# Seven-product groups and GpSimd lower parts in the down projection of a two-layer encoder trunk

## The chip, the cores and the metric

The kernel runs on one core of a Trainium2 chip. A core has a matrix engine (TensorE, PE in the profile; PEld is its weight load), a vector engine (VectorE, DVE), an activation engine (ScalarE, ACT), a general engine (GpSimd, POOL) and a queue engine that starts most transfers (SyncE, SP). Matmuls accumulate in PSUM, eight banks of 128 x 512 float32 values; everything else lies in SBUF. The metric is the time of one execution on the device in microseconds.

## The reference

The input is one sequence of 256 tokens with 2048 features. There are two layers. Layer 0 mixes tokens with a convolution module, layer 1 with latent attention. After each comes the same MLP:

```
def sq_relu_mlp(h, w1, w2):
    return jnp.square(jax.nn.relu(h @ w1)) @ w2

    for layer in range(DEPTH):
        h = rms_norm(x, norm_mixer_g[layer])
        x = x + (conv_module(h, ...) if layer % 2 == 0 else mla(h, ...))
        h = rms_norm(x, norm_mlp_g[layer])
        x = x + sq_relu_mlp(h, mlp_w1[layer], mlp_w2[layer])
    return rms_norm(x, final_norm_g)
```

All tensors are float32. `mlp_w1` is 2048 x 8192 and `mlp_w2`, the down projection, 8192 x 2048, for each layer.

## The kernel before

**Products in three terms.** TensorE multiplies in a reduced format (`F32R`). To keep float32's accuracy each operand is split into an upper part (`hi`, a rounding copy on ScalarE, L168 and L489) and a lower part (`lo = raw - hi`, a subtraction, L172 and L490). A product is then three matmuls, `hi*hi + lo*hi + hi*lo` (`mm3`, L201 to L203). Every weight that comes from memory therefore passes through ScalarE and one more engine before TensorE can use it. `load` fetches a block of weights of 512 KB or 1 MB into one of three `raw` buffers; `split` makes the two parts in two halves of 128 x 1024, in rings of six `hi` and six `lo` buffers (`WB`).

**The MLP** (`mlp`) handles the 8192 inner features in two halves. A half has an up stage and a down stage. The up stage makes eight groups of 512 inner features: matmuls at L615 and L616, then the squared ReLU on VectorE (L634 to L637) and its split into `gh`, `gl`. The down stage multiplies these with `mlp_w2`, for two blocks of 512 output columns at a time (`Sums`, here called a column pair), and adds the result to the residual `xs`. Each half has two column pairs, so the kernel has eight.

**Plain and mixed groups.** A plain pair of 128-row chunks of the inner dimension, against two row tiles of tokens and two column blocks, takes 8 products, 24 matmuls (`Sums.plain`). A mixed pair takes 7 products, 21 matmuls (`Sums.mixed`), after Strassen's scheme in Winograd's form. For that the weights are combined first (`mixed_weights`): VectorE makes one subtraction of 128 x 1024 (L497) and two of 128 x 512 (L498, L499) on the raw weights, and seven matrices have to be split instead of four: three lower parts of 1024 columns and one of 512, all on VectorE (L490). The activations are combined likewise in the up stage (`mixed_inputs`). `MIXED` names the mixed groups of each layer and half: 0, 2, 4 in three of them, 0 and 2 in layer 0's second half. They have buffers of a larger shape (`sh`, `sl`, `N_MIXED` of each).

**Order.** A column pair holds all eight PSUM banks: four shared sums `u` and four ends `e`. Mixed and plain pairs alternate while there are mixed ones; then come the rest of the plain ones. Ahead of the last plain pair stands `join`, which combines the `u` banks into the residual: one copy on ScalarE and eight additions on VectorE. The last column pair of a half is run differently (`product_A` with `beside=between`): there the plain groups come as blocks of four chunks by 512 columns, and in the very last stage the last block's last three groups are worked through once per row tile, so that the first tile's final norm can begin early (`finish`, `before`). `turns_on` takes a few small steps from a list (transposes of the residual on VectorE for the next layer's input) behind each pair. The engines work through their queues in order; the order of the MLP's instructions is made by a scheduler from the order of the program.

**Elsewhere.** In the convolution stage the lower parts of `conv_w_pw1` are made by GpSimd (L172), and so are some additions; VectorE sums filter taps there, with the running sum in PSUM (L848). In the attention GpSimd turns the rotary part of the queries (L1317 to L1322, L1530). `w_dw`, the table of filter taps, lies in the pool of constants; `gf`, the final gain, has a pool of its own that is open during the last MLP.

Of the kernel before, what the change touches and what calls it, by code (L numbers as in the profile page):

```python
# [10 lines left out]
F32 = mybir.dt.float32  # L11
# [4 lines left out]
ALU = mybir.AluOpType  # L16
AX = mybir.AxisListType

P = 128
D = 2048  # L20
# [13 lines left out]
KR = 512  # L34
CHUNK = 64
HALVES = 2
PAD_CONST = 24
PAD_SMALL = 48
PAD_RIGHT = 48
PAD_KV = 8  # L40
PAD_O = 56
WB = 6
LOOK = WB // 2 - 1
MIXED = {(0, 0): (0, 2, 4), (0, 1): (0, 2), (1, 0): (0, 2, 4), (1, 1): (0, 2, 4)}
N_MIXED = 3


SIDE = {KC - 3: 2, KC - 2: 4}
# [29 lines left out]
def trunk_kernel(  # L78
# [323 lines left out]

    def product_A(
        w, k_lo, nk, hi, lo, add, prepare, blocks=range(NNB), due=(), finish=None, before=None,
        groups=None, banks=None, begun=None, beside=None,
    ):

        due = list(due)
        groups = list(range(nk // 4)) if groups is None else groups
        begun = set() if begun is None else begun  # L410
        nu = len(groups)

        def first(ps):
            fresh = id(ps) not in begun
            begun.add(id(ps))
            return fresh

        for n in blocks:
            ps = [acc_tile() for _ in range(T)] if banks is None else banks[n]

            n_end = 3 if finish is not None and n == blocks[-1] else 0
            wjs = []

            def products(u, t, to_end=True):
                for j in range(4):
                    mm3(
                        ps[t], hi(4 * groups[u] + j, t), lo(4 * groups[u] + j, t), *wjs[u](j),
                        first(ps[t]), u == nu - 1 - (not to_end) and j == 3,
                    )

            for u, g in enumerate(groups):
                wjs.append(load_split([rows(w, k_lo + 4 * g, 4, n * NB, NB)], 4))
                if u < nu - n_end:
                    for j in range(4):
                        k = 4 * g + j
                        for t in range(T):
                            mm3(ps[t], hi(k, t), lo(k, t), *wjs[u](j), first(ps[t]), u == nu - 1 and j == 3)
                if banks is None:
                    while due:
                        prepare(due.pop(0))  # L440
                    step(-(-20 * 4 // nk) + 1 if nk > 4 * NNB else 6)
                else:
                    turns_on(due, prepare)
                if u == 0 and n_end:
                    before()
                if beside is not None:
                    beside(n, u, due)
            if n_end:
                for t in range(T):


                    halves = t == T - 1
                    for u in range(nu - n_end, nu - halves):
                        products(u, t, not halves)
                    add(n, ps, t)
                    if not halves:
                        prepare(n, t)
                    else:
                        h = NB // 2
                        for c in range(2):  # L460
                            o = acc_tile()[:, :h]
                            for j in range(4):
                                k = 4 * groups[-1] + j
                                wh, wl = (w[:, c * h : (c + 1) * h] for w in wjs[-1](j))
                                mm3(o, hi(k, t), lo(k, t), wh, wl, j == 0, j == 3)
                            add(n, {t: o}, t, c)
                            prepare(n, t, c)
                    finish(t)
            else:
                for t in range(T):  # L470
                    add(n, ps, t)
                due.append(n)
        while due:
            prepare(due.pop(0))

    def turns_on(due, prepare, n=4):

        if due and not steps:
            prepare(due.pop(0))
        step(n)  # L480
# [42 lines left out]
    class Sums:  # L523
# [25 lines left out]

        def plain(self, w, k, hi, lo, k0, end):  # L550

            at_j = split(load([rows(w, k, 2, self.n * NB, 2 * NB)], 2), nc.vector)
            order = [(j, c, t) for j in range(2) for c in range(2) for t in range(T)]
            if end:
                order.sort(key=lambda r: r[1:])
            for j, c, t in order:
                wh, wl = (a[:, c * NB : (c + 1) * NB] for a in at_j(j))
                ps = self.e[t][c]
                mm3(ps, hi(k0 + j, t), lo(k0 + j, t), wh, wl, self.first(ps), end and j == 1)

        def join(self, pool):

            u1, u6, u7, u5 = self.u
            x = lambda t, c: xs[:, t, (self.n + c) * NB : (self.n + c + 1) * NB]
            a, b = (pool.tile([P, 2, S], F32, tag="v", name=nm("v"), bufs=2).rearrange("p a n -> p (a n)") for _ in range(2))
            tt = nc.vector.tensor_tensor
            nc.scalar.activation(a, u1, AF.Copy)
            tt(x(0, 0), u1, x(0, 0), op=ALU.add)
            tt(a, u6, a, op=ALU.add)
            tt(b, u7, a, op=ALU.add)  # L570
            tt(a, u5, a, op=ALU.add)
            tt(x(1, 0), b, x(1, 0), op=ALU.add)
            tt(b, u5, b, op=ALU.add)
            tt(x(0, 1), a, x(0, 1), op=ALU.add)
            tt(x(1, 1), b, x(1, 1), op=ALU.add)

    def mlp(layer, ssq, next_gain, finish=None, before=None, beside=None):

        with ExitStack() as cx:
            mp = cx.enter_context(tc.tile_pool(name=f"mp{layer}", bufs=1, reuse_waits="tile"))  # L580
# [16 lines left out]
            for hf in range(HALVES):  # L597
# [4 lines left out]
                for g in range(ng):  # L602
# [17 lines left out]
                    if beside is not None and g == 2:  # L620
                        beside(mp)
                        beside = None
                    if g in mixed or len(mixed) < N_MIXED and g == plain[-1]:
                        shape = [P, 2, 7, P] if g in mixed else [P, 4, S]
                        gs[g] = [mp.tile(shape, F32R, tag=f"s{c}", name=nm(f"s{c}"), bufs=N_MIXED) for c in "hl"]
                    else:
                        gs[g] = [mp.tile([P, 4, S], F32R, tag=f"g{c}", name=nm(f"g{c}"), bufs=ng - N_MIXED) for c in "hl"]
# [29 lines left out]
                for n in range(0, NNB - 2 * last, 2):  # L657
                    sums = Sums(n)
                    ks = [4 * g + 2 * b for g in plain for b in range(2)]
                    for i, k in enumerate(ks):  # L660
                        if i < len(ms):
                            mixed_quad(sums, i)
                            turns_on(due, prepare)
                        if i == len(ks) - 2:
                            sums.join(mp)
                        sums.plain(w, k_lo + k, hi, lo, k, i == len(ks) - 1)
                        turns_on(due, prepare)
                    for c in range(2):
                        for t in range(T):
                            add(n + c, [sums.e[i][c] for i in range(T)], t)  # L670
                        if last:
                            due.append(n + c)
                if last:
# [2 lines left out]

                    def between(n, u, due):
                        if n == n2 and u < len(plain) - 1:
                            lo_i, hi_i = (len(ms) * i // (len(plain) - 1) for i in (u, u + 1))
                            for i in range(lo_i, hi_i):  # L680
                                mixed_quad(sums, i)
                                turns_on(due, prepare)
                        if n == n2 and u == len(plain) - 1:
                            sums.join(mp)

                    product_A(
                        w, k_lo, nkh, hi, lo, add, prepare, range(n2, NNB), due,
                        finish=(lambda t: finish(nssq, t)) if finish is not None else None,
                        before=lambda: before(nssq),
                        groups=plain, banks={n2 + c: [sums.e[t][c] for t in range(T)] for c in range(2)},  # L690
                        begun=sums.begun, beside=between,
                    )
            return nssq

# [1 line left out]
    with ExitStack() as cx:  # L696
# [1 line left out]
        cv2 = cx.enter_context(tc.tile_pool(name="cv2", bufs=2, reuse_waits="tile"))  # L698

        NW = W * KC // 4  # L700
        w_dw = const.tile([P, W * KC], F32, name="w_dw")

        X_PARTS = [(0, D // 2, 3 * D // 4, D), (0, D // 2, 7 * D // 8, D)]
        X_PARTS = [list(zip(c, c[1:])) for c in X_PARTS]
# [1055 lines left out]
        product_A(mla_w_o[0], 0, H, oh_kt, ol_kt, add, prepare, range(2, NNB), range(2))  # L1760


    with tc.tile_pool(name="fin", bufs=1, reuse_waits="tile") as fp:
        gf = fp.tile([P, D], F32, name="gf")
        nc.scalar.dma_start(gf, final_norm_g.rearrange("(a n) -> a n", a=1).partition_broadcast(P))

        def gained(t, n):
            sl = slice(n * NB, (n + 1) * NB)
            nc.vector.tensor_tensor(xs[:, t, sl], xs[:, t, sl], gf[:, sl], op=ALU.mult)

        def finish(ssq, t):

# [17 lines left out]
            for i, (c0, c1) in enumerate(zip(cuts, cuts[1:])):  # L1790
                ob = xs[:, t, c0:c1]
                if c1 == D:
                    nc.vector.scalar_tensor_tensor(
                        out=ob, in0=ob, scalar=y, in1=gf[:, c0:c1], op0=ALU.mult, op1=ALU.mult
                    )
                elif i in (1, 3):
                    nc.scalar.activation(ob, ob, AF.Copy, scale=y)
# [20 lines left out]
                for n in range(NNB - 1):  # L1818
                    gained(t, n)

        mlp(1, ssq, None, finish, before)


_INS = [
# [23 lines left out]
```

## Time and profile before

| what | us |
|---|---|
| median of 3 runs | 1955.66 (1955.34 to 1955.98) |
| profiled execution | 1955.42 |
| its span, from the first to the last instruction | 1953.6 |
| TensorE busy | 1932.2 |
| VectorE busy | 1547.1 |
| ScalarE busy | 1058.6 |
| GpSimd busy | 220.5 |

The granted TensorE clock was 0.998. A row of the groups names line, engine, operation, output and inputs, shape and count, then busy time, the mean of one in ns, and the idle time of the engine just before such instructions with what ended it. A row of the order of time has start and length in us, engine, line, operation, operands, count, and in brackets the idle time ahead of it. A matmul's own length is its latency; as they are pipelined, the distance from one to the next is shorter.

### The profile page before, as it was taken

The numbers are of one execution on the slowest core, as the hardware profiler recorded it, in microseconds if no ns is written. First come the engines' busy times: TensorE is split into PE (matmuls) and PEld (weight loads), VectorE is DVE, ScalarE is ACT, GpSimd is POOL, SyncE is SP. The second block draws the span as 40 slices with busy tenths as digits, with TensorE's granted clock in tenths as the row PEclk, the third lists the DMA queues.
The fourth block names the chain that finished last, engine by engine and source line by source line (L and its number), as shares of the span: only waits on it lengthen the run. The fifth ranks groups of instructions, "written<-read, shape, count | busy, mean of one in ns | idle before, by whom it ended". The sixth has DMA issues, their size and how long they took to land. (4 is left out here: it accounts for less than half of the span.)

```text
span 1953.6 us, 28331 instructions
## 1 busy us (share of the span) xinstructions
PE 1932.2 (99%) x10835; PEld 1691.2 (87%) x10835; DVE 1547.1 (79%) x2400; ACT 1058.6 (54%) x1568; POOL 220.5 (11%) x172
## 2 busy tenths in 40 slices
PE   8999999999999999999999999999999999999998
PEld 8999888888888888888789998888888888888886
DVE  7999988877988676787966665876788876778896
ACT  5667755554645454454556665555555545455554
POOL 6999100000000000000001310000000000000000
PEclk9999999999999999999999999999999999999999
DMA  7765556664657666564565445566656566664754
GB/s 231 209 192 175 169 180 212 194 187 159 225 191 231 191 185 188 169 231 157 172 193 173 120 144 180 173 223 189 192 171 217 193 222 190 193 193 160 237 168 147
DMA packets 216746, 367.62 MB, mean 188 GB/s; under 512 B 15513, under 2 KB 90529, under 8 KB 216353
## 3 DMA queue, kind: packets, MB, share of 16 engines
q1 hardware_dynamic: 215280, 363.28, 58.7%
q10 hardware_dynamic: 1328, 2.52, 0.4%
q8 instruction: 85, 1.39, 0.3%
q14 instruction: 53, 0.43, 0.1%
HBM read 363.68 MB, written 2.10 MB: 187 GB/s over the span
## 5 line engine op out<-in xcount | busy, mean ns | idle before, releaser
L172 DVE TENSOR_TENSOR lo<-raw,hi 128x1024 fp32r<-128x1024 f32 (+2 forms) x543 | 647.9, 1205 | 294.7 <-ACT hi L168 290.8
L168 ACT ACTIVATE hi<-raw 128x1024 fp32r<-128x1024 f32 (+2 forms) x608 | 622.8, 1040 | 462.6 <-PE acc L615 238.7
L615 PE MATMUL acc<-xt,hi 128*128 128x512 f32 x2048 | 710.5, 390 | 0.0
L616 PE MATMUL acc<-xt,lo 128*128 128x256 f32 x2048 | 577.5, 282 | 0.0
L615 PEld LDWEIGHTS acc<-xt,hi 128*128 128x128 f32 x2048 | 384.4, 188 | 80.6
L616 PEld LDWEIGHTS acc<-xt,lo 128*128 128x128 f32 x2048 | 387.1, 189 | 0.2
L489 ACT ACTIVATE hi<-raw 128x1024 fp32r<-128x1024 f32 (+1 forms) x176 | 164.0, 949 | 179.8 <-DVE raw L497 70.1
L203 PE MATMUL acc<-lo,gh 128*128 128x512 f32 (+1 forms) x644 | 250.2, 388 | 1.1 <-DVE lo L172 0.9
L201 PE MATMUL acc<-hi,gh 128*128 128x512 f32 (+1 forms) x644 | 249.7, 388 | 0.0
L202 PE MATMUL acc<-hi,gl 128*128 128x512 f32 (+1 forms) x644 | 249.7, 388 | 0.0
L490 DVE TENSOR_TENSOR lo<-raw,hi 128x1024 fp32r<-128x1024 f32 (+1 forms) x176 | 188.5, 1087 | 34.2 <-ACT hi L489 30.6
L761 PE MATMUL acc<-xt,hi 128*128 128x256 f32 x1024 | 180.1, 281 | 0.3 <-ACT b L1043 0.2
L848 DVE SCALAR_TENSOR_TENSOR sum<-ub,w_dw,sum 128x256 f32<-128x256 f32 x409 | 164.2, 480 | 3.5 <-ACT sum L818 3.0
L203 PE MATMUL acc<-lo,sh 128*128 128x512 f32 x404 | 157.8, 391 | 2.8 <-DVE lo L490 2.6
L201 PE MATMUL acc<-hi,sh 128*128 128x512 f32 x404 | 157.4, 390 | 0.0
L172 POOL TENSOR_TENSOR lo<-raw,hi 128x1024 fp32r<-128x1024 f32 x65 | 154.9, 2408 | 17.3 <-ACT hi L168 17.3
L761 PEld LDWEIGHTS acc<-xt,hi 128*128 128x128 f32 x1024 | 154.6, 188 | 1.1 <-ACT xt L1027 0.6
L203 PEld LDWEIGHTS acc<-lo,gh 128*128 128x128 f32 x644 | 120.9, 188 | 27.5 <-DVE lo L172 2.7
L201 PEld LDWEIGHTS acc<-hi,gh 128*128 128x128 f32 x644 | 120.9, 188 | 24.8
L202 PEld LDWEIGHTS acc<-hi,gl 128*128 128x128 f32 x644 | 120.9, 188 | 24.7
L761 PE MATMUL acc<-xt,lo 128*128 128x256 f32 x512 | 139.2, 279 | 0.0
L202 PE MATMUL acc<-hi,sl 128*128 128x512 f32 x340 | 132.4, 389 | 0.0
(310 smaller groups left out, 2359.5 us busy)
## 6 DMA issues: line engine op xcount, KB each, us to landing
raw<-in_mlp_w SPq DMA_DIRECT2D x256, 1024.0 KB, 5.4
raw<-in_conv_w_pw SPq DMA_DIRECT2D x62, 512.0 KB, 5.1
raw<-in_conv_w_pw SPq DMA_DIRECT2D x16, 1024.0 KB, 5.1
raw<-in_mla_w_o SPq DMA_DIRECT2D x16, 1024.0 KB, 5.6
raw<-in_mla_w_kv_up SPq DMA_DIRECT2D x8, 1024.0 KB, 5.5
raw<-in_mla_w_in SPq DMA_DIRECT2D x8, 576.0 KB, 3.7
raw<-in_mla_w_in SPq DMA_DIRECT2D x4, 1024.0 KB
raw<-in_mla_w_q_up SPq DMA_DIRECT2D x16, 256.0 KB, 3.3
```

The costliest lines, as they stand in the source:

```text
L168: nc.scalar.activation(hi, raw[:, js, :], AF.Copy)
L172: eng.tensor_tensor(lo, raw, hi.bitcast(F32), op=ALU.subtract)
L201: nc.tensor.matmul(ps, sh, mh, start=start, stop=False)
L202: nc.tensor.matmul(ps, sl, mh, start=False, stop=False)
L203: nc.tensor.matmul(ps, sh, ml, start=False, stop=stop)
L489: nc.scalar.activation(hi, src, AF.Copy)
L490: nc.vector.tensor_tensor(lo, src, hi.bitcast(F32), op=ALU.subtract)
L615: nc.tensor.matmul(ps[b], wh[:, bs], xhl(k), start=k == 0, stop=False)
L616: nc.tensor.matmul(ps[b][:, :S], wl[:, bs], xh(k), start=False, stop=k == KC - 1)
L761: nc.tensor.matmul(pss[c][b][:, :S], w[i][:, bs], (xh, xl)[j](k), start=k == i + j == 0, stop=end and k == k0 + nk - 1 and (i, j) == terms ...
L848: nc.vector.scalar_tensor_tensor(out=out, in0=ubs[c][:, w : w + S], scalar=tap(c, w), in1=base, op0=ALU.mult, op1=ALU.add)
```

## The change

1. Half of the groups, four of eight, are mixed in three of the four halves: 0, 2, 4, 6 (`MIXED`, `N_MIXED`). Layer 0's second half keeps 0 and 2.
2. The lower parts of the plain pairs in the down stages are made by GpSimd (`nc.gpsimd` in `Sums.plain`, `eng` in `product_A`). The mixed pairs' stay on VectorE.
3. In `join` three of the eight additions, those from SBUF into the residual, go to GpSimd, through `scratch` for the third.
4. The mixed pairs are spread over the plain ones so that the last `TAIL` plain pairs follow all of them: M M P M P M P M M P M P M P P P in place of six times M P and four P more. In the last column pair of a half the first mixed pairs now come ahead of the first plain group (`beside(n, -1, due)`).
5. `turns_on` takes three or six steps instead of four.
6. `w_dw` moves from the constants to the convolution's pool; `gf` moves to the place of the normed inputs `xt` and is loaded after the last up stage; a pad of constants is smaller.

```diff
-PAD_CONST = 24
+PAD_CONST = 8
...
-MIXED = {(0, 0): (0, 2, 4), (0, 1): (0, 2), (1, 0): (0, 2, 4), (1, 1): (0, 2, 4)}
-N_MIXED = 3
+MIXED = {(0, 0): (0, 2, 4, 6), (0, 1): (0, 2), (1, 0): (0, 2, 4, 6), (1, 1): (0, 2, 4, 6)}
+N_MIXED = 4
+TAIL = 3
...
             for u, g in enumerate(groups):
-                wjs.append(load_split([rows(w, k_lo + 4 * g, 4, n * NB, NB)], 4))
+                if u == 0 and beside is not None:
+                    beside(n, -1, due)
+                wjs.append(split(load([rows(w, k_lo + 4 * g, 4, n * NB, NB)], 4), eng or nc.vector))
...
-                    turns_on(due, prepare)
+                    turns_on(due, prepare, 3 if n == blocks[0] else 6)
...
-    def turns_on(due, prepare, n=4):
+    def turns_on(due, prepare, n=3):
...
-            at_j = split(load([rows(w, k, 2, self.n * NB, 2 * NB)], 2), nc.vector)
+            at_j = split(load([rows(w, k, 2, self.n * NB, 2 * NB)], 2), nc.gpsimd)
...
             tt(a, u5, a, op=ALU.add)
-            tt(x(1, 0), b, x(1, 0), op=ALU.add)
-            tt(b, u5, b, op=ALU.add)
-            tt(x(0, 1), a, x(0, 1), op=ALU.add)
-            tt(x(1, 1), b, x(1, 1), op=ALU.add)
+            tt(scratch, u5, b, op=ALU.add)
+            for (t, c), o in (((1, 0), b), ((0, 1), a), ((1, 1), scratch)):
+                nc.gpsimd.tensor_tensor(x(t, c), o, x(t, c), op=ALU.add)
...
-                    if g in mixed or len(mixed) < N_MIXED and g == plain[-1]:
+                    if g in mixed or g in plain[len(plain) + len(mixed) - N_MIXED :]:
...
+                    at = 0
                     for i, k in enumerate(ks):
-                        if i < len(ms):
-                            mixed_quad(sums, i)
+                        upto = -(-len(ms) * (i + 1) // (len(ks) - TAIL + 1))
+                        while at < min(upto, len(ms)):
+                            mixed_quad(sums, at)
                             turns_on(due, prepare)
+                            at += 1
...
-                            lo_i, hi_i = (len(ms) * i // (len(plain) - 1) for i in (u, u + 1))
+                            lo_i, hi_i = (len(ms) * i // len(plain) for i in (u + 1, u + 2))
...
+                    if after_up is not None:
+                        after_up()
...
-                        begun=sums.begun, beside=between,
+                        begun=sums.begun, beside=between, eng=nc.gpsimd,
...
-        w_dw = const.tile([P, W * KC], F32, name="w_dw")
+        w_dw = cv.tile([P, NB], F32, name="w_dw")[:, : W * KC]
...
-        gf = fp.tile([P, D], F32, name="gf")
-        nc.scalar.dma_start(gf, final_norm_g.rearrange("(a n) -> a n", a=1).partition_broadcast(P))
+        def load_gf():
+            gfs.append(right_pool("gf", 1).tile([P, D], F32, name="gf"))
+            nc.scalar.dma_start(gfs[0], final_norm_g.rearrange("(a n) -> a n", a=1).partition_broadcast(P))
...
-        mlp(1, ssq, None, finish, before)
+        mlp(1, ssq, None, finish, before, after_up=load_gf)
```

More of the change, by code (lines that the diff above doesn't have):

```diff
@@ L404, in product_A @@
         w, k_lo, nk, hi, lo, add, prepare, blocks=range(NNB), due=(), finish=None, before=None,
-        groups=None, banks=None, begun=None, beside=None,
+        groups=None, banks=None, begun=None, beside=None, eng=None,
     ):
@@ L571, in join, with mlp @@
             tt(a, u5, a, op=ALU.add)
-            tt(x(1, 0), b, x(1, 0), op=ALU.add)
-            tt(b, u5, b, op=ALU.add)
-            tt(x(0, 1), a, x(0, 1), op=ALU.add)
-            tt(x(1, 1), b, x(1, 1), op=ALU.add)
-    def mlp(layer, ssq, next_gain, finish=None, before=None, beside=None):
+            tt(scratch, u5, b, op=ALU.add)
+            for (t, c), o in (((1, 0), b), ((0, 1), a), ((1, 1), scratch)):
+                nc.gpsimd.tensor_tensor(x(t, c), o, x(t, c), op=ALU.add)
+    def mlp(layer, ssq, next_gain, finish=None, before=None, beside=None, after_up=None):
         with ExitStack() as cx:
@@ L1760, in trunk_kernel @@
         product_A(mla_w_o[0], 0, H, oh_kt, ol_kt, add, prepare, range(2, NNB), range(2))
-    with tc.tile_pool(name="fin", bufs=1, reuse_waits="tile") as fp:
-        gf = fp.tile([P, D], F32, name="gf")
-        nc.scalar.dma_start(gf, final_norm_g.rearrange("(a n) -> a n", a=1).partition_broadcast(P))
+    with ExitStack():
+        gfs = []
+        def load_gf():
+            gfs.append(right_pool("gf", 1).tile([P, D], F32, name="gf"))
+            nc.scalar.dma_start(gfs[0], final_norm_g.rearrange("(a n) -> a n", a=1).partition_broadcast(P))
         def gained(t, n):
             sl = slice(n * NB, (n + 1) * NB)
-            nc.vector.tensor_tensor(xs[:, t, sl], xs[:, t, sl], gf[:, sl], op=ALU.mult)
+            nc.vector.tensor_tensor(xs[:, t, sl], xs[:, t, sl], gfs[0][:, sl], op=ALU.mult)
         def finish(ssq, t):
@@ L1793, in finish @@
                     nc.vector.scalar_tensor_tensor(
-                        out=ob, in0=ob, scalar=y, in1=gf[:, c0:c1], op0=ALU.mult, op1=ALU.mult
+                        out=ob, in0=ob, scalar=y, in1=gfs[0][:, c0:c1], op0=ALU.mult, op1=ALU.mult
                     )
```

## The prediction

> **What bounds the kernel now.** I read the page's busy table first, then the windows cut at the borders of the stages, then TensorE's waits, then the groups by line and the order of time inside one down stage.
>
> ```profile
> span 1953.6 us, 28331 instructions
> PE 1932.2 (99%) x10835; PEld 1691.2 (87%) x10835; DVE 1547.1 (79%) x2400; ACT 1058.6 (54%) x1568; POOL 220.5 (11%) x172
> ```
>
> TensorE is the bound; GpSimd is nearly free. The profiled execution took 1955.42 us, 0.24 below the median of the runs, so I make the sum against 1955.4.
>
> The windows of the first MLP's up stage and of the four down stages (layer 0 halves 0 and 1, layer 1 halves 0 and 1); the columns are the window, its length, then each engine's busy us:
>
> ```profile
> core 0: us, PE busy (x) PEld busy (x) DVE busy (x) ACT busy (x) POOL busy (x), PEclk, DMA share, GB/s
> 322.00:478.00 156.00, 156.00 (x903) 138.33 (x902) 118.89 (x195) 80.24 (x117) 0.00 (x0) 1.00 0.59 184
> 478.00:644.00 166.00, 166.00 (x734) 137.43 (x733) 142.61 (x153) 87.58 (x94) 0.00 (x0) 1.00 0.64 209
> 821.00:998.00 177.00, 172.81 (x754) 139.71 (x754) 151.21 (x196) 89.46 (x115) 0.18 (x2) 1.00 0.57 187
> 1435.00:1601.00 166.00, 166.00 (x735) 137.54 (x734) 143.12 (x154) 87.45 (x96) 0.00 (x0) 1.00 0.64 209
> 1779.00:1945.00 166.00, 166.00 (x745) 137.83 (x743) 143.97 (x169) 88.04 (x108) 0.00 (x0) 1.00 0.56 187
> ```
>
> In three down stages TensorE never stops: 734 matmuls in 166.0 us, 0.226 us each (its mean of 0.39 is latency of a pipelined instruction). Only layer 0's second half loses time: 744 matmuls would take 168, it takes 177. VectorE is busy for 143 of 166, GpSimd does nothing. So there is little left but fewer matmuls, and the price is paid by whoever prepares the weights. TensorE's waits in that half, with how often and the longest, name them already:
>
> ```profile
> PE acc L203 <- DVE lo L490: 2.6, 2, 1.6
> PE acc L203 <- DVE lo L172: 0.9, 1, 0.9
> ```
>
> **The change, part by part.**
>
> *Fewer matmuls.* A mixed pair of chunks needs 21 matmuls, a plain pair 24. One more mixed group in three of the four halves is 3 groups x 2 pairs x 2 column pairs = 12 pairs, 36 matmuls: 36 x 0.226 = 8.1 us off TensorE, which is what the change could win if nothing else bound it.
>
> *Preparation of the weights.* Order of time on VectorE inside layer 0's first down stage, one mixed pair and one plain pair:
>
> ```profile
> 502.63 1.81 DVE L490 TENSOR_TENSOR lo<-raw,hi 128x1024 fp32r<-128x1024 f32 x2
> 504.37 1.22 DVE L497 TENSOR_TENSOR raw<-raw 128x1024 f32<-128x1024 f32 x1
> 505.62 0.69 DVE L498 TENSOR_TENSOR raw<-raw 128x512 f32<-128x512 f32 x1
> 506.34 0.69 DVE L499 TENSOR_TENSOR raw<-raw 128x512 f32<-128x512 f32 x1
> 506.95 2.52 DVE L490 TENSOR_TENSOR lo<-raw,hi 128x1024 fp32r<-128x1024 f32 x2
> 509.39 2.35 DVE L172 TENSOR_TENSOR lo<-raw,hi 128x1024 fp32r<-128x1024 f32 x2
> 511.66 1.82 DVE L490 TENSOR_TENSOR lo<-raw,hi 128x1024 fp32r<-128x1024 f32 x2
> ```
>
> A mixed pair costs VectorE 509.39 - 502.63 = 6.76 us, a plain pair 2.27 (1.14 for each lower part when they follow each other). Before: 9.0 us for one of each, against (21 + 24) x 0.226 = 10.2 on TensorE; hidden. After, the plain pair's two lower parts are GpSimd's. On paper VectorE falls to 6.76 per couple and GpSimd works beside it. GpSimd's durations for the same form, in the convolution stage:
>
> ```profile
> L172 POOL TENSOR_TENSOR lo<-raw,hi 128x1024 fp32r<-128x1024 f32 x65 | 154.9, 2408 | 17.3 <-ACT hi L168 17.3
> L845 POOL TENSOR_TENSOR half<-half,tp x15: 732/749/774, 42.7 to 199.5; 128x256 f32<-128x256 f32 x15
> L848 DVE SCALAR_TENSOR_TENSOR sum<-ub,w_dw,sum x409: 473/480/490, 29.1 to 205.2; 128x256 f32<-128x256 f32 x137
> ```
>
> There both engines ran side by side undisturbed (spread under 4% on VectorE), but VectorE's instructions there read one operand from PSUM. The lower part reads both operands (raw and hi) from SBUF, and so do all seven VectorE instructions of a mixed pair. The one place where such instructions meet GpSimd's work is the rotary part of the attention:
>
> ```profile
> 1064.21 0.46 POOL L1319 TENSOR_TENSOR m<-scratch,cos 128x128 f32<-128x128 f32 x1
> 1064.64 1.44 POOL L1320 TENSOR_TENSOR m<-scratch,sin 128x128 f32<-128x128 f32 x1
> 1066.04 1.44 POOL L1321 TENSOR_TENSOR qp<-m,m 128x128 f32<-128x128 f32 x1
> ...
> 1068.80 0.46 POOL L1318 TENSOR_TENSOR m<-scratch,sin 128x128 f32<-128x128 f32 x1
> ```
>
> ```profile
> 1064.28 2.88 DVE L172 TENSOR_TENSOR lo<-raw,hi 128x1024 fp32r<-128x1024 f32 x2 [1.68 <-ACT hi L168]
> 1086.63 1.21 DVE L172 TENSOR_TENSOR lo<-raw,hi 128x512 fp32r<-128x512 f32 x1
> ```
>
> ```profile
> 1086.52 0.78 POOL L1530 TENSOR_TENSOR qhl<-qp,qhl 128x256 fp32r<-128x256 f32 x1
> ```
>
> A GpSimd instruction of 0.46 us takes 1.44 beside a lower part: it waits for the whole of it. The other way round, the 512-column lower part at 1086.63 started 0.11 after GpSimd's 0.78 and took 1.21, where the 512-column instructions above take 0.69. The two engines take turns. One turn of each, from 1064.64 to 1066.04, takes 1.40 us for a 1024-column lower part and a 128-column GpSimd instruction.
>
> The Trainium skill, SBUF — State Buffer, section Who interferes with whom, states this as a rule: a VectorE instruction with two SBUF inputs and a GpSimd instruction that reads SBUF use one shared read interface, and the later one is blocked until the earlier has finished. Taken to the letter it makes the couple below 6.76 + 2 x 2.41 = 11.6 us instead of 11.2, an estimate that adds 3 us per column pair.
>
> From the rows: a GpSimd lower part of 1024 columns is 2.41 - 0.46 = 1.95 us longer than the 128-column instruction, so a turn of both is 1.40 + 1.95 = 3.35. A couple (mixed and plain pair) then needs two such turns and the rest of VectorE's work alone: 2 x 3.35 + 6.76 - 2 x 1.14 = 11.2 us, more than TensorE's 10.2. The cover is gone. For unknown ends: nothing blocked leaves 10.2 (TensorE); to the full GpSimd duration with nothing gained at the hand-over, 6.76 + 2 x 2.41 = 11.6; 11.2 stands nearest to the rows, which show real turns.
>
> *The joins.* Three additions of 512 columns go to GpSimd: between 0.75 (256) and 2.41 (1024) lies 1.30; in turns that is 1.40 - 1.14 + 1.30 - 0.46 = 1.1 each, 3.3 per column pair. VectorE's other nine (join and adds) read PSUM and run beside GpSimd. GpSimd's queue holds the join ahead of the next lower parts, so these wait for VectorE's join, and it for the last mixed matmul.
>
> *Sum per stage.* Layer 0 first half and layer 1 first half: 8 couples x 11.2 + 3.3 = 93 per column pair, where TensorE took 83 before; two of them 186. Off: the first mixed pair and a part of the next are ready when the stage begins, 8 us (six hi/lo buffers; VectorE has slack in the up stage, 119 of 156). On: 4 where the second column pair begins with two mixed pairs and VectorE's adds stand between them, 3 for the last matmuls. 185 against 166 is +19, less 1 for waits in which GpSimd slips in: +18 each.
>
> Layer 1's second half: 93 for the first column pair; then 8 mixed and 3 plain pairs up to the last mixed matmul, 8 x 6.76 + 3 x (11.2 - 6.76) = 67; with 4 - 8 again, 156. Behind it stand 120 matmuls, 27 us. In that tail each group of the last block is used by only 12 matmuls (2.7 us) in the first row tile, while GpSimd makes a group in 4.8; join and four groups are 3.9 + 19, of which the first lies ahead; I get 35. Together 191 against 166: +25.
>
> Layer 0's second half keeps two mixed groups: 4 x 6.76 + 12 x 4.44 + 3.3 = 84 per column pair, TensorE 84. It loses its present 9 us and gains them again by a port at 100% beside 48 transposes of VectorE: 0, from -8 to +15.
>
> *Mixed inputs* of three more groups: some 6 us of VectorE in each up stage, hidden by its 37 idle. *The rest at nothing:* the smaller constant pad, the tap table in a pool of the convolution, the final gain loaded over the finished inputs on ScalarE's queue behind work long done; each lies beside 20 us or more of matmuls, and if the gain came late it would cost its landing, some 5 us (a weight of the same size lands in 5.4):
>
> ```profile
> raw<-in_mlp_w SPq DMA_DIRECT2D x256, 1024.0 KB, 5.4
> ```
>
> The 8.1 us are in these numbers already, as the stages are no longer counted by matmuls. 1955.4 + 18 + 18 + 25 + 0 = 2016 us.
>
> **The rivals.**
>
> *Faster.* GpSimd's longer instruction does not hold VectorE out for its whole length (the trace shows only instructions up to 0.78 us). It decides where one costs VectorE less than (10.2 - 6.76) / 2 = 1.7 us: then TensorE stays the bound, the 8.1 us come, and the 9 us of waits in layer 0's second half shrink by some 5: 1942. For it speaks that each engine's own sum fits; against it that even the 256-column instruction blocked VectorE to its end. 0.08.
>
> *A milder port.* Waits between VectorE's dependent instructions (504.37 to 505.62 is 1.25 for 1.14 of work) let GpSimd in: 10.6 per couple, 88 per column pair, some 5 less in each of six, and layer 0's second half gains 7: 1980. 0.24.
>
> *A harder one.* Lower parts that end later hold the three raw buffers longer, so the next load starts later; with 5.4 us to land and some 12 of contended use, two loads per couple over three buffers just fit 11.2. Where they don't, a couple takes 12: six column pairs x 6.4, and layer 0's second half +10: 2064. 0.16.
>
> **How the numbers follow.** Main case 0.50 (1995 to 2040), milder 0.24, harder 0.16, faster 0.08, and 0.02 for cancelling out. What a measurement can tell is 0.2%, 4 us. Slower 0.90, same 0.02, faster 0.08. The range runs from 1970, below the milder case, to 2062, near the harder one.
>
> **What would show it.** TensorE's busy share falls to 95-96%, with waits for lower parts of VectorE and GpSimd in the three stages with four mixed groups, each some 18 to 25 us longer; 36 matmuls fewer; mean lower part of VectorE in the mixed pairs well over 1.22 us and GpSimd's over 2.41 (3 or more). It is wrong if the windows show TensorE busy throughout with GpSimd at 2.41 beside VectorE at 1.22, or if the loss lies in the tail alone.

## The result, and the profile after

The changed kernel takes 2048.54 us (2048.29 to 2049.48) against 1955.82 us: a ratio of 1.0475, 95% interval 1.0456 to 1.0493. It is slower by 93 us. The prediction was 2016, range 1970 to 2062: the sign, the cause and the range held, the size was two thirds of what came, and 2048.5 lies above the main case's own 1995 to 2040.

The page's head and busy table after:

```profile
span 2046.5 us, 28548 instructions
PE 1963.8 (96%) x10799; PEld 1678.2 (82%) x10799; DVE 1563.1 (76%) x2328; ACT 1072.9 (52%) x1604; POOL 643.8 (31%) x340
```

The 36 matmuls are gone (10835 to 10799). TensorE is down to 96% all the same; VectorE has fewer instructions and yet more busy time (1547.1 before). The windows of the four down stages after, columns as before:

```profile
478.30:669.50 191.20, 175.77 (x723) 133.59 (x722) 154.17 (x132) 90.39 (x101) 99.01 (x38) 0.99 0.54 173
846.90:1030.70 183.80, 174.24 (x754) 139.36 (x754) 124.67 (x143) 88.35 (x116) 124.00 (x56) 1.00 0.55 178
1467.70:1658.90 191.20, 175.77 (x723) 133.56 (x722) 153.61 (x132) 90.50 (x101) 99.01 (x38) 0.99 0.53 173
1836.20:2038.70 202.50, 176.96 (x734) 132.19 (x732) 152.58 (x152) 93.16 (x116) 95.88 (x38) 1.00 0.48 158
```

| stage | before | after | difference | predicted |
|---|---|---|---|---|
| layer 0, first half | 166.0 | 191.2 | +25.2 | +18 |
| layer 0, second half | 177.0 | 183.8 | +6.8 | 0 |
| layer 1, first half | 166.0 | 191.2 | +25.2 | +18 |
| layer 1, second half | 166.0 | 202.5 | +36.5 | +25 |

The four differences, 94 us, make up the whole loss. In the first stage VectorE is busy for 154.17 us with 132 instructions; before, it was 142.61 with 153. So single instructions became longer. What TensorE waited for (total, times, longest):

```profile
PE acc L204 <- POOL lo L173: 35.0, 56, 2.0
PE acc L204 <- DVE lo L493: 17.4, 25, 1.6
PE acc L202 <- ACT hi L492: 10.3, 15, 1.0
```

All three are parts of weights. One couple of a mixed and a plain pair in the order of time, VectorE and then GpSimd (L493 is the old L490, L500 to L502 the old L497 to L499, L173 the old L172):

```profile
502.35 4.53 DVE L493 TENSOR_TENSOR lo<-raw,hi 128x1024 fp32r<-128x1024 f32 x2 [1.62 <-PE acc L203]
506.80 1.21 DVE L500 TENSOR_TENSOR raw<-raw 128x1024 f32<-128x1024 f32 x1
508.05 0.69 DVE L501 TENSOR_TENSOR raw<-raw 128x512 f32<-128x512 f32 x1
508.77 0.69 DVE L502 TENSOR_TENSOR raw<-raw 128x512 f32<-128x512 f32 x1
509.38 2.52 DVE L493 TENSOR_TENSOR lo<-raw,hi 128x1024 fp32r<-128x1024 f32 x2
513.52 4.54 DVE L493 TENSOR_TENSOR lo<-raw,hi 128x1024 fp32r<-128x1024 f32 x2 [1.62 <-ACT hi L492]
```

```profile
500.50 5.83 POOL L173 TENSOR_TENSOR lo<-raw,hi 128x1024 fp32r<-128x1024 f32 x2 [5.34 <-ACT hi L169]
511.67 5.84 POOL L173 TENSOR_TENSOR lo<-raw,hi 128x1024 fp32r<-128x1024 f32 x2 [5.34 <-ACT hi L169]
```

The first two lower parts, of 1024 and 512 columns, took VectorE 1.81 us before and take 4.53 now: while GpSimd's 5.83 us run, VectorE gets one turn between the two and otherwise stands inside an instruction. GpSimd's pair takes 5.83 where two alone take 4.8. The couple repeats every 513.52 - 502.35 = 11.17 us. By form, the 512-column lower part in the first stage before, and then the same and GpSimd's in the first stage after:

```profile
L490 DVE TENSOR_TENSOR lo<-raw,hi 128x512 fp32r<-128x512 f32 x11 | 7.5, 683 | 0.0
```

```profile
L493 DVE TENSOR_TENSOR lo<-raw,hi 128x512 fp32r<-128x512 f32 x15 | 33.3, 2220 | 0.0
L173 POOL TENSOR_TENSOR lo<-raw,hi 128x1024 fp32r<-128x1024 f32 x32 | 88.7, 2800 | 364.9 <-ACT hi L169 364.9
```

The 512-column lower part has gone from 683 ns to a mean of 2220, GpSimd's from 2408 (in the convolution stage before) to 2800.

### The profile page after: what moved, and what is told of

Same layout as the page of the kernel before. It is cut to its first block, busy times and chain, and to the rows that moved or that the text cites. A ratio compares the mean times of both kernels' runs of the same rounds, so it can differ in the third digit from the quotient of the medians.

```text
span 2046.5 us, 28548 instructions
## 1 busy us (share of the span) xinstructions
PE 1963.8 (96%) x10799; PEld 1678.2 (82%) x10799; DVE 1563.1 (76%) x2328; ACT 1072.9 (52%) x1604; POOL 643.8 (31%) x340
## 5 line engine op out<-in xcount | busy, mean ns | idle before, releaser
L173 POOL TENSOR_TENSOR lo<-raw,hi 128x1024 fp32r<-128x1024 f32 x209 | 536.7, 2595 | 1264.0 <-ACT hi L169 1201.9
L169 ACT ACTIVATE hi<-raw 128x1024 fp32r<-128x1024 f32 (+1 forms) x584 | 593.1, 1038 | 377.2 <-PE acc L617 225.6
L173 DVE TENSOR_TENSOR lo<-raw,hi 128x1024 fp32r<-128x1024 f32 (+1 forms) x375 | 455.8, 1225 | 239.5 <-ACT hi L169 235.6
L493 DVE TENSOR_TENSOR lo<-raw,hi 128x1024 fp32r<-128x1024 f32 x224 | 326.2, 1474 | 133.5 <-ACT hi L492 124.2
L492 ACT ACTIVATE hi<-raw 128x1024 fp32r<-128x1024 f32 x224 | 206.2, 946 | 313.5 <-DVE raw L500 206.3
L204 PE MATMUL acc<-lo,sh 128*128 128x512 f32 x520 | 206.9, 401 | 20.6 <-DVE lo L493 17.4
L202 PE MATMUL acc<-hi,sh 128*128 128x512 f32 x520 | 207.1, 398 | 11.1 <-ACT hi L492 10.3
L203 PE MATMUL acc<-hi,gl 128*128 128x512 f32 (+1 forms) x516 | 200.6, 389 | 0.0
L204 PEld LDWEIGHTS acc<-lo,sh 128*128 128x128 f32 x520 | 97.9, 189 | 55.6 <-DVE lo L493 32.0
L202 PEld LDWEIGHTS acc<-hi,sh 128*128 128x128 f32 x520 | 98.3, 189 | 40.3 <-ACT hi L492 19.7
```

What stands on the lines that cost most here:

```text
L169: nc.scalar.activation(hi, raw[:, js, :], AF.Copy)
L173: eng.tensor_tensor(lo, raw, hi.bitcast(F32), op=ALU.subtract)
L202: nc.tensor.matmul(ps, sh, mh, start=start, stop=False)
L203: nc.tensor.matmul(ps, sl, mh, start=False, stop=False)
L204: nc.tensor.matmul(ps, sh, ml, start=False, stop=stop)
L492: nc.scalar.activation(hi, src, AF.Copy)
```

## The experiments

**The theories.** The port theory is the prediction's: VectorE and GpSimd take turns at reading when both have two operands in SBUF. Rivals: the lateness theory (GpSimd's lower parts are only twice as long and come late), and that the fourth group or the new order costs the time. Times below are medians, beside the kernel before in the same comparison (1955.1 to 1955.4 us).

**All lower parts of the down stages on VectorE**, the rest as changed:

```diff
-            at_j = split(load([rows(w, k, 2, self.n * NB, 2 * NB)], 2), nc.gpsimd)
+            at_j = split(load([rows(w, k, 2, self.n * NB, 2 * NB)], 2), nc.vector)
...
-                        begun=sums.begun, beside=between, eng=nc.gpsimd,
+                        begun=sums.begun, beside=between,
```

> The changed kernel with the plain pairs' lower parts back on VectorE in the down stages; four mixed groups, the new order and GpSimd's three additions per join stay. Port theory (GpSimd and VectorE take turns at reading two SBUF operands): VectorE needs 6.76 + 2.27 = 9.0 us per couple of a mixed and a plain pair, below TensorE's 10.2, so the waits go and the 36 matmuls come off: about 1950 us (1944 to 1965). Lateness theory (GpSimd's lower parts are only long and come late, the port matters little): the same, about 1950. Rival that the fourth mixed group or the new order costs the time: still above 2020.

1956.35 us, ratio 1.0005 (0.9996 to 1.0015). 92 of the 93 us hang on the engine of those lower parts; without it the fourth group and the new order cost nothing on balance. The time lies in the range that both theories gave, so it does not tell them apart. But the 8 us of the 36 matmuls do not come either. By stage it gains 5 us in layer 0's second half and loses 6.5 in the very last; see below.

**Useless reads by GpSimd**, on top of the last kernel:

```diff
-            at_j = split(load([rows(w, k, 2, self.n * NB, 2 * NB)], 2), nc.vector)
+            raw = load([rows(w, k, 2, self.n * NB, 2 * NB)], 2)
+            at_j = split(raw, nc.vector)
+            for j in range(2):
+                used = raw[:, j, :NB]
+                nc.gpsimd.tensor_tensor(used, used, used, op=ALU.add)
```

> As the run with all lower parts on VectorE, with one useless GpSimd addition of 128x512 behind each lower part of a plain pair, over raw weights that are used up: no matmul waits for it, and it reads SBUF. Port theory: each takes 1.1 us of VectorE's turn, 9.0 + 2 x 1.1 = 11.2 us per couple, so some 8 us per column pair in six of them: about 1995 us (1980 to 2020), with VectorE's two-operand instructions much longer than 1.22 in part. Lateness theory: nothing that TensorE needs is later, so within 10 us of the run with all lower parts on VectorE.

2002.31 us, ratio 1.0240 (1.0220 to 1.0261): inside the port theory's range, far outside the lateness theory's.

**Fills in the same place:**

```diff
-                used = raw[:, j, :NB]
-                nc.gpsimd.tensor_tensor(used, used, used, op=ALU.add)
+                nc.gpsimd.memset(raw[:, j, :], 0.0)
+                nc.gpsimd.memset(raw[:, j, :NB], 0.0)
```

> As the last one, with two GpSimd fills (128x1024 and 128x512) of the used-up raw weights in place of each addition: the same place in the queues, the same hold on the raw buffers, nothing read. Port theory with the read interface as the shared part: within 10 us of the run with all lower parts on VectorE. If the raw buffers' later release is what costs, it comes out as slow as the run with additions; if GpSimd's writes share the port too, likewise.

1957.12 us, ratio 1.0010 (1.0000 to 1.0020). GpSimd and VectorE by form from 478 to 640 us, in the first down stage, first with the reads, then with the fills:

```profile
L559 POOL TENSOR_TENSOR raw<-raw 128x512 f32<-128x512 f32 x26 | 51.1, 1985 | 375.1 <-DVE lo L173 375.1
L493 DVE TENSOR_TENSOR lo<-raw,hi 128x1024 fp32r<-128x1024 f32 x43 | 61.0, 1425 | 3.7 <-ACT hi L492 2.9
L493 DVE TENSOR_TENSOR lo<-raw,hi 128x512 fp32r<-128x512 f32 x15 | 19.5, 1300 | 0.0
```

```profile
L558 POOL MEMSET raw<- 128x1024 f32 x32 | 30.6, 957 | 377.3 <-DVE lo L173 377.3
L559 POOL MEMSET raw<- 128x512 f32 x32 | 16.9, 527 | 1.6
L493 DVE TENSOR_TENSOR lo<-raw,hi 128x1024 fp32r<-128x1024 f32 x44 | 53.5, 1221 | 5.0 <-ACT hi L492 4.1
L493 DVE TENSOR_TENSOR lo<-raw,hi 128x512 fp32r<-128x512 f32 x15 | 11.3, 757 | 0.0
```

Work that nobody needs costs 46 us when it reads and 1 us when it only writes, though two fills, 957 + 527 ns, hold GpSimd and the raw buffer a little longer than an addition that meets no turn (1.29 us for that form in the last stage of the changed kernel). That is the port theory's forecast, and the lateness theory has nothing here that could be late. So GpSimd's reads beside VectorE's two-operand work are shown to suffice for a loss of 46 us, half of the 93. The Trainium skill, SBUF — State Buffer, section Who interferes with whom, makes the same difference: a VectorE instruction with two SBUF inputs contends with GpSimd's reads and not with its writes. The traces agree, 1425 and 1300 ns against 1221 and 757.

The additions, stretched to 1985 ns, do hold the raw buffer half a microsecond longer than the fills. In the couples that is not what costs, as ScalarE waits for no load there. The couple's period, from one L500 to the next, first with the reads, then with the fills:

```profile
494.62 1.21 DVE L500 TENSOR_TENSOR raw<-raw 128x1024 f32<-128x1024 f32 x1
505.35 1.21 DVE L500 TENSOR_TENSOR raw<-raw 128x1024 f32<-128x1024 f32 x1
```

```profile
493.03 1.22 DVE L500 TENSOR_TENSOR raw<-raw 128x1024 f32<-128x1024 f32 x1
502.06 1.22 DVE L500 TENSOR_TENSOR raw<-raw 128x1024 f32<-128x1024 f32 x1
```

10.7 us with the reads, where 11.2 was expected, is above TensorE's 10.2; 9.0 with the fills is VectorE's own work and stays hidden.

**Half of the lower parts on GpSimd:**

```diff
-        parts = [split_half(raw, h, eng) for h in range(2)]
+        parts = [split_half(raw, h, nc.vector if h == 0 else eng) for h in range(2)]
```

> The changed kernel with the first of the two lower parts of a plain block on VectorE and the second on GpSimd. Port theory: 6.76 + 1.14 + 2.2 = 10.1 us per couple, just at TensorE's 10.2: most of the loss goes, 1955 to 1975 us. Lateness theory: half of the lower parts are late, about half of the loss stays, near 2000.

1995.36 us, ratio 1.0205 (1.0185 to 1.0225): the port theory's time was missed, the lateness theory's met. The couple itself came out as the port theory has it:

```profile
501.06 3.46 DVE L493 TENSOR_TENSOR lo<-raw,hi 128x1024 fp32r<-128x1024 f32 x2 [0.48 <-ACT hi L492]
511.16 3.46 DVE L493 TENSOR_TENSOR lo<-raw,hi 128x1024 fp32r<-128x1024 f32 x2 [0.48 <-ACT hi L492]
```

10.10 us against 10.1 forecast, just under TensorE's 10.2. What was probably missed is that a couple at 10.1 leaves no slack: where two mixed pairs follow each other (6.8 us each on VectorE, 4.8 on TensorE) the wait can't be made up. No run took those places out. TensorE's waits for weights are for VectorE's and ScalarE's parts here, and hardly for GpSimd's:

```profile
PE acc L204 <- DVE lo L493: 12.8, 23, 1.6
PE acc L202 <- ACT hi L492: 10.4, 13, 1.0
PE acc L204 <- DVE lo L173: 5.1, 2, 3.0
PE acc L204 <- POOL lo L173: 0.5, 1, 0.5
```

If late GpSimd parts made this kernel slow, the last row would be the largest. So the lateness theory met the time without its cause.

**The kernel before with nothing but those lower parts on GpSimd:**

```diff
-            at_j = split(load([rows(w, k, 2, self.n * NB, 2 * NB)], 2), nc.vector)
+            at_j = split(load([rows(w, k, 2, self.n * NB, 2 * NB)], 2), nc.gpsimd)
...
-                wjs.append(load_split([rows(w, k_lo + 4 * g, 4, n * NB, NB)], 4))
+                wjs.append(split(load([rows(w, k_lo + 4 * g, 4, n * NB, NB)], 4), eng or nc.vector))
...
-                        begun=sums.begun, beside=between,
+                        begun=sums.begun, beside=between, eng=nc.gpsimd,
```

> The kernel before with one edit: the plain pairs' lower parts of the down stages on GpSimd; three mixed groups, order and joins as before. Port theory: six couples of 11.2 and four plain pairs of 5.4 (TensorE) are 89 us per column pair instead of 83; with the half that has two mixed groups about even and some 8 us more in the last tail, 1990 us (1975 to 2010). If the loss needs the fourth group or the new order, under 1965.

2005.42 us, ratio 1.0255 (1.0235 to 1.0276). That is inside the port theory's range, and the couple has the 11.17 us of the changed kernel. So neither the fourth group nor the new order is needed for a loss: that edit alone costs 50 us. With the fourth group, the new order and GpSimd's additions in the joins beside it, it is 93; which of them adds how much was not separated, apart from the joins below.

**The last column pairs' plain blocks back on VectorE:**

```diff
-                        begun=sums.begun, beside=between, eng=nc.gpsimd,
+                        begun=sums.begun, beside=between,
```

> The changed kernel with the lower parts of the plain blocks in each half's last column pair back on VectorE, those of the other column pairs still on GpSimd. The tail step of the prediction (GpSimd makes a group in 4.8 us where TensorE uses it up in 2.7) gives some 10 us back there, and as much in the rest of that stage: about 2028 us (2020 to 2036). If the tail is bound by something else, within 4 us of 2048.

2028.91 us, ratio 1.0376 (1.0355 to 1.0396), as forecast: 20 us hang on the last column pairs' lower parts. Only the second half of each layer ends in such a column pair (`product_A`), so there are two in the kernel, not four.

**The joins back on VectorE:**

```diff
-            tt(scratch, u5, b, op=ALU.add)
-            for (t, c), o in (((1, 0), b), ((0, 1), a), ((1, 1), scratch)):
-                nc.gpsimd.tensor_tensor(x(t, c), o, x(t, c), op=ALU.add)
+            tt(x(1, 0), b, x(1, 0), op=ALU.add)
+            tt(b, u5, b, op=ALU.add)
+            tt(x(0, 1), a, x(0, 1), op=ALU.add)
+            tt(x(1, 1), b, x(1, 1), op=ALU.add)
```

> The changed kernel with all eight additions of a join on VectorE again. By the trace of the changed kernel the first mixed pair of the next column pair is prepared beside the three GpSimd additions and its instructions are 3 us longer there; without them that goes, and VectorE has 1.8 us more to do itself: 1.5 to 3.5 us less per column pair in eight, 2030 us (2020 to 2040). The prediction's 3.3 us per column pair would give 2022. If the joins cost nothing, 2048.

2040.10 us, ratio 1.0434 (1.0414 to 1.0454): 8 us, or 1.1 per column pair, a third of the prediction's 3.3 and less than the 1.5 to 3.5 expected here. It is not spread evenly: the first half's stage of each layer gains 0.6 us (191.2 to 190.6), layer 0's second half 2.7, the very last stage 4.0 (202.5 to 198.5).

**The buffers alone**, in the kernel before:

```diff
-PAD_CONST = 24
+PAD_CONST = 8
...
-        w_dw = const.tile([P, W * KC], F32, name="w_dw")
+        w_dw = cv.tile([P, NB], F32, name="w_dw")[:, : W * KC]
...
-        nc.scalar.dma_start(gf, final_norm_g.rearrange("(a n) -> a n", a=1).partition_broadcast(P))
+            nc.scalar.dma_start(gfs[0], final_norm_g.rearrange("(a n) -> a n", a=1).partition_broadcast(P))
```

> The kernel before with nothing but the buffers moved: the smaller pad, the tap table in the convolution's pool, the final gain loaded after the last up stage. The prediction put these at nothing: within 2 us of the kernel before. If the gain came late it would cost up to 5 us.

1955.12 us, ratio 0.9999 (0.9990 to 1.0009): nothing, as the prediction put it.

**Getting the matmuls' gain.** Three kernels with all lower parts on VectorE. First two plain pairs at the end in place of three:

```diff
-TAIL = 3
+TAIL = 2
```

> As the run with all lower parts on VectorE, with two plain pairs behind the last mixed one in place of three, so that two mixed pairs follow each other once in a column pair instead of twice. VectorE needs 6.8 us for a mixed pair and TensorE 4.8, so each such place costs a wait where nothing is prepared ahead: 1952 us (1947 to 1957).

1959.23 us, ratio 1.0020 (1.0011 to 1.0030): a miss, 3 us worse than three at the end. Its first stage took 166.8 us against 165.7, so on balance the shorter tail costs more than one place fewer with two mixed pairs saves. Then, on top, three mixed groups in the very last half:

```diff
-MIXED = {(0, 0): (0, 2, 4, 6), (0, 1): (0, 2), (1, 0): (0, 2, 4, 6), (1, 1): (0, 2, 4, 6)}
+MIXED = {(0, 0): (0, 2, 4, 6), (0, 1): (0, 2), (1, 0): (0, 2, 4, 6), (1, 1): (0, 2, 4)}
```

> As the last one, with three mixed groups in place of four in the very last half, whose last column pair sets two mixed pairs ahead of each plain block (15.8 us on VectorE for 15.0 on TensorE). That half gains back the 6.5 us that it had lost against the kernel before: 1947 us (1943 to 1953), faster than the kernel before by some 8 us if the other waits stay as they are.

1951.49 us, ratio 0.9980 (0.9971 to 0.9990). The last half's stage falls from 173.9 to 166.2 us. The same with three plain pairs at the end:

```diff
-TAIL = 2
+TAIL = 3
```

> All lower parts of the down stages on VectorE, four mixed groups in two halves, three in the very last, two in layer 0's second, with three plain pairs behind the last mixed one. The down stages as in the runs before: 165.6 + 172 + 165.6 + 166.2 us: 1949 us (1946 to 1953), 2 us below the same with two plain pairs at the end.

1949.13 us, ratio 0.9969 (0.9958 to 0.9981). And with the joins on VectorE (the edit above):

> As the last one, with all eight additions of a join on VectorE. VectorE has 1.2 us of slack per couple, and the additions stand ahead of three plain pairs: within 3 us of the last one.

1948.86 us, ratio 0.9968 (0.9955 to 0.9980). Both beat the kernel before by 6 us (0.3%; both intervals lie below 1) and the changed one by 100. Busy table of the first of the two:

```profile
PE 1927.2 (99%) x10811; PEld 1686.5 (87%) x10811; DVE 1581.5 (81%) x2440; ACT 1069.7 (55%) x1592; POOL 268.4 (14%) x196
```

It has 24 matmuls fewer than the kernel before, 5.4 us at 0.226; about as much is gained in layer 0's second half (177.0 to 172.4 us) and some 2 us are lost again in each of the two stages with four mixed groups (165.7 us where 720 matmuls at 0.227 are 163.4), probably where mixed pairs follow each other. What makes layer 0's second half faster, the new order or the smaller steps, was not separated.

## Why the prediction was right, and where its sum was not

- *TensorE has no idle time to win back; the matmuls are 36 fewer.* Both as predicted.
- *The couple needs 11.2 us.* Measured 11.17. The composition differs: the formula took two whole turns; the trace shows VectorE held for 2.7 us and idle for 1.6, waiting for an upper part. ScalarE in the same couple:

```profile
508.13 1.06 ACT L492 ACTIVATE hi<-raw 128x1024 fp32r<-128x1024 f32 x1 [5.29 <-DVE raw L500]
509.58 1.06 ACT L492 ACTIVATE hi<-raw 128x1024 fp32r<-128x1024 f32 x1 [0.39 <-DVE raw L502]
510.55 1.99 ACT L169 ACTIVATE hi<-raw 128x1024 fp32r<-128x1024 f32 x2
512.45 1.56 ACT L492 ACTIVATE hi<-raw 128x1024 fp32r<-128x1024 f32 x2
```

  ScalarE stands for 5.29 us until VectorE's L500 is done, and makes the next mixed pair's first upper part only behind the plain pair's two (L169). VectorE from 502.35 to the end of its L502 at 509.47, then ScalarE from 509.58 to 513.49, make up the 11.17 us: a loop of the two engines, in which nothing waits for TensorE (the 1.62 us at 502.35 are put down to TensorE, but ScalarE's part came only 0.04 us ahead of the start). Without the 2.7 us of turns it would take some 8.5 us, an estimate from these rows, and hide under TensorE's 10.2. So by this reading it is the turns that cost in the couples, and TensorE's waits for GpSimd's parts there follow from them. The agreement to 0.03 us is therefore partly luck; the half dose (10.10 for 10.1) carries the price of a single turn better.
- *Two column pairs are 186, less 8 that are ready at the start, plus 4 and 3.* This is the step that was mis-sized: 185 became 191.2. The start, the boundary between the column pairs, and the tail of plain pairs all went another way. Against 720 matmuls at 0.227 us TensorE loses 27.8 us in this stage: 4 of them lie ahead of 496 us, 6.4 between 574 and 589, around the boundary (1.6 of these at the lower clock shown at the end), the rest in the couples, the tails and the places where mixed pairs follow each other. VectorE and GpSimd around the boundary in the first stage after:

```profile
553.09 15.25 POOL L173 TENSOR_TENSOR lo<-raw,hi 128x1024 fp32r<-128x1024 f32 x6 [5.35 <-ACT hi L169]
568.30 3.98 POOL L577 TENSOR_TENSOR xs<-v,xs 128x512 f32<-128x512 f32 x2
572.24 1.74 POOL L577 TENSOR_TENSOR xs<-scratch,xs 128x512 f32<-128x512 f32 x1
```

```profile
564.42 1.68 DVE L493 TENSOR_TENSOR lo<-raw,hi 128x1024 fp32r<-128x1024 f32 x1 [6.51 <-ACT hi L492]
566.20 3.22 DVE L500 TENSOR_TENSOR raw<-raw 128x1024 f32<-128x1024 f32 x1
569.34 1.79 DVE L493 TENSOR_TENSOR lo<-raw,hi 128x512 fp32r<-128x512 f32 x1
571.17 1.66 DVE L501 TENSOR_TENSOR raw<-raw 128x512 f32<-128x512 f32 x1
572.86 1.66 DVE L502 TENSOR_TENSOR raw<-raw 128x512 f32<-128x512 f32 x1
574.44 2.51 DVE L493 TENSOR_TENSOR lo<-raw,hi 128x1024 fp32r<-128x1024 f32 x2
```

  While GpSimd makes the six lower parts of the last three plain pairs, VectorE is idle for 6.5 us, waiting for the next mixed pair's upper parts, and those wait for a late load:

```profile
555.54 2.40 POOL L173 TENSOR_TENSOR lo<-raw,hi 128x1024 fp32r<-128x1024 f32 x1
557.97 0.37 SPq L159 DMA_DIRECT2D raw<-in_mlp_w  x1
563.33 1.58 ACT L492 ACTIVATE hi<-raw 128x1024 fp32r<-128x1024 f32 x2 [2.56 <-DMA raw<-in_mlp_w]
```

  SyncE starts it when GpSimd's second lower part, ending at 557.94, frees the raw buffer, and ScalarE can make the upper parts only when it has landed. Then that mixed pair takes 564.42 to 576.9, 12.5 us instead of 6.76, beside GpSimd's last lower part and its three additions of the join. The sum had credited preparation ahead; here the two engines took no turns for 6.5 us and then both wanted theirs at once. TensorE is busy for 12.6 of the next 16 us (574 to 590).
- *Layer 1's second half, +25:* +36.5. Up to the last mixed matmul (2001.7) it took some 165 us for a predicted 156, in which 8 us of work ahead were credited as well; the tail behind it took some 37 us for a predicted 35 (GpSimd's last six lower parts run alone from 2014.2 to 2029.2). Of the 20 us that the last column pairs gain with VectorE, 14 lie in this stage (202.5 to 188.4).
- *Layer 0's second half, 0 (from -8 to +15):* +6.8, inside.
- *The joins, 3.3 per column pair:* 1.1 by experiment, most of it in the two second halves, 2.7 and 4.0 us, against 0.6 in each first half. In the very last stage the three additions, 2010.5 to 2014.2, stand ahead of GpSimd's last six lower parts.
- *Buffers, mixed inputs, the gain at nothing:* right; the up stages are unchanged.
- *The rivals.* "Faster" fell: GpSimd's long instruction does hold VectorE to its end. Its price, 1942, was not tested: the run at 1956 has no lower part on GpSimd, but gives VectorE the plain pairs' 2.27 us per couple as well. "Harder" was near in time (2064), but its couple of 12 us, for loads that start late, did not come: the couple stayed at 11.17 and waits for no load. At the boundary above a load does start late, and in the first stage ScalarE waits 12.7 us for loads in all (2.8 before). The fills, which held the raw buffers too, cost 1 us. "Milder", 10.6 per couple, fell with the 11.17.
- *The signs.* TensorE at 96%, waits for lower parts of both engines and 36 matmuls fewer were seen. GpSimd's lower part took 2.80 us where 3 or more was named. VectorE's of 1024 columns in the mixed pairs took 1.35 on average, little over 1.22; the length sits in the 512-column ones, 2.22 us.
- *Still open:* outside the couples, how much of the 93 us is the turns and how much GpSimd's parts being late for TensorE, 35 us of whose waits are named after them. No run made them late without reading. The price of the mixed and plain pairs' order under the port was not taken apart either.

## What to carry to other kernels

Before work is moved to an idle GpSimd, look at what VectorE reads beside it: with two SBUF operands on both sides the two engines took turns here, and a couple that hid 9.0 us of VectorE under 10.2 of TensorE needs 11.2. The profile shows the turns as longer instructions and not as idle time (2.7 us of a couple), so compare the mean of the same form in two windows. And a scheme with fewer matmuls pays only while its preparation keeps pace at every place. Leave it out where the pairs would follow each other too closely: in the last half here, three mixed groups in place of four saved nearly 8 us.

## What had not been expected of the hardware

After a few short stops TensorE ran at about half speed for a while. Behind the boundary shown above, one window and the matmuls in it:

```profile
584.00:590.00 6.00, 5.32 (x17) 4.09 (x17) 4.33 (x4) 4.18 (x5) 4.10 (x2) 0.72 0.46 137
```

```profile
585.20 0.63 PE L202 MATMUL acc<-hi,sh 128*128 128x512 f32 x1
585.63 0.63 PE L203 MATMUL acc<-hi,sl 128*128 128x512 f32 x1
586.06 0.63 PE L204 MATMUL acc<-lo,sh 128*128 128x512 f32 x1
```

The granted clock is 0.72 over these 6 us, and matmuls start every 0.43 us instead of 0.226, for 3.4 us. No stop ahead of it was longer than 1.6 us. It happened twice in the run while TensorE had work, at 1.6 us each, so it explains at most 3 of the 93 us. No run shows what sets it off; if it is the stops, a stage in which TensorE often waits a little can pay a second time.
